# Strassen-like matmul with GELU on one core: the input check moved to settled blocks, transposes that read runs, a GELU issued one row tile later

## The chip, the core and the metric

The kernel runs on one core of a Trainium2 chip. The metric is the device time of one execution in microseconds (us); lower is better. The core has a matrix engine (TensorE, PE), a vector engine (VectorE, DVE), a scalar engine (ScalarE, ACT), GpSimd (POOL) and SyncE (SP). Each works through its own queue in order, and they wait for each other by semaphores. GpSimd and SyncE issue the DMA transfers here: GpSimd the loads, which turn float32 into 16-bit floats on the way, and SyncE the stores.

## The reference

```python
def setup_inputs():
    m, k, n = 4096, 4096, 4096
    return {
        "a": np.random.randn(m, k).astype(np.float32),
        "b": np.random.randn(k, n).astype(np.float32),
    }

def reference(a, b):
    x = np.matmul(a, b)
    return 0.5 * x * (1 + np.tanh(np.sqrt(2 / np.pi) * (x + 0.044715 * x**3)))
```

## The kernel before

`half_path` multiplies in float16 with one level of Winograd's form of Strassen's scheme: A, B and the output are each cut into four quadrants ("11", "12", "21", "22"), and seven products of quadrants or of sums of quadrants (`PRODUCTS`, L30) take the place of eight. If a check of the inputs says that their size does not suit float16, `general_path` (L49) computes everything again in bfloat16; with the inputs here it does not run.

**Groups, products, steps.** The output's quadrants are cut into four row blocks (`mb`) of 512 rows and four column blocks (`nb`) of 512 columns. A pair of them is a group, 16 in all, with `nb` the same from the last group of a row block to the first of the next, so that between them only A's blocks change (`groups`, L259). A group runs products 0 to 6, a product has four steps `q` of a quarter of the inner length, and a step has 16 matmuls: four row tiles `i` by four pieces of 128. So a step is 16 matmuls, a product 64, a group 448. Products 1 to 4 gather in the PSUM banks `accX`, products 0, 5 and 6 in `accY`, one bank for each row tile.

**Operands.** `make_sums` (L244) builds with VectorE, two steps ahead of the matmuls, the sums `aS` and `bS` of quadrants (128x2048, float16) for those products that need sums; there are three buffers of each. `settle` (L309), called behind each row tile of a product's last step, takes the result out. At product 1 `keep` copies the bank to `m5` with ScalarE, VectorE makes y = Y - m5, and `emit` (L296) applies GELU with ScalarE and stores y with SyncE. Product 2 goes on in the same banks, so its first matmul into bank `i` waits for the copy of row tile `i`. At product 5 and 6 VectorE makes y out of bank Y and a kept block, and `emit` follows.

**Loads and turns.** `load_a` (L125) brings 512 rows by 1024 columns of A into one of two staging buffers (`stage`) with four DMAs of 32 partitions; `turn_a` (L137) turns it with one VectorE transpose of 4-byte elements (pairs of float16) into `aT`, reading with a step of four elements, and squares every one of its 16 pieces of 256 columns on ScalarE, with a running sum into `stat_a`: the check of A. So a staging buffer is read by VectorE and by ScalarE. `load_b` (L151) brings 1024 rows by 512 columns of B into `bR` with one DMA of 128 partitions. Every DMA of GpSimd takes one of eight semaphores in turn and waits until the DMA eight before it has landed.

**The order.** It is written out by hand: `at(gi, s, q, fn, ...)` hangs a call ahead of a step (L341), and the loop at L430 issues for each step those calls, the sums of the step two later, and the step's matmuls. The first group's loads and turns are listed at L351 to L367; the later ones come from the loop at L378, B's for the next group in its products 3, 4 and 6, A's for the next row block from product 4 of the row block's last group to product 3 of the next. In the second group of each row block `square_b` squares B's blocks on ScalarE, VectorE adds the squares (`add_squares`), and `weigh_b` takes their largest, smallest and total. In the last row block `ask` gathers the figures to DRAM ahead of product 0 of the group before the last, `answer` brings them back in one row and forms the verdict ahead of product 3 there, and `read` loads it into a register of every engine ahead of product 0 of the last group.

Of the kernel before, what the change touches and what calls it, by code (L numbers as in the profile page):

```python
# [16 lines left out]
P = 128  # L17
Q = 32
# [25 lines left out]
A_LOW, A_RATIO = 2.0**-8, 16.0  # L44
B_LOW, B_RATIO = 2.0**-13, 64.0
# [43 lines left out]
def half_path(  # L89
# [21 lines left out]
    n_seg = M * K // (P * RUN)  # L111
    stat_a = pool.tile([P, n_seg], F32, name="stat_a", tag="stat_a")
    stat_b = pool.tile([P, 3, 2 * NNB], F32, name="stat_b", tag="stat_b")
    segments = iter(range(n_seg))
    checks = iter(range(2 * NNB))

    a_v = a.rearrange("(x mm) (c g r) -> c g mm x r", mm=Q, g=4, r=RUN)
    b_v = b.rearrange("(c p j) n -> c p j n", p=P, j=NJ)
# [18 lines left out]
    def turn_a(mb, quad, c):  # L137
        s = staged.pop((mb, quad, c))
        t = pool.tile([P, NJ // 2, TM * 2], F16, name="aT", tag=f"aT{a_slot[quad]}{c}")
        src = s.bitcast(U32).rearrange("p mb (q jj) -> p jj mb q", q=Q)  # L140
# [3 lines left out]
        for x in range(TM // Q):  # L144
            k = next(segments)
            junk = pool.tile([P, RUN], BF16, name="junk", tag="junk")
            nc.scalar.activation(  # L147
                junk[:, :], s[:, x, :], ACT.Square, accum_out=stat_a[:, k : k + 1]
            )

    def load_b(nb, quad, c):  # L151
        kh, jh = int(quad[0]) - 1, int(quad[1]) - 1
        n0 = jh * NH + nb * NC
        t = pool.tile([P, NJ, NC], F16, name="bR", tag=f"bR{b_slot[quad]}{c}")
        nc.gpsimd.dma_start(out=t[:, :, :], in_=b_v[kh * CH + c, :, :, n0 : n0 + NC])  # L155
        b_tiles[nb, quad, c] = t
# [7 lines left out]
    energy, squares = {}, {}  # L164
    W = 2 * NC

    def square_b(nb, quad, c, h):

        src = b_tiles[nb, quad, c].rearrange("p x y -> p (x y)")[:, h * W : (h + 1) * W]
        half = quad[1]  # L170
        if half not in energy:
            t = energy[half] = pool.tile([P, W], BF16, name="energy", tag=f"energy{half}")
        else:
            t = pool.tile([P, W], BF16, name="square", tag="square", bufs=2)
            squares.setdefault(half, []).append(t)
        nc.scalar.activation(t[:, :], src, ACT.Square)  # L176

    def add_squares():
        for half in squares:
            for t in squares[half]:  # L180
                tt(energy[half], energy[half], t, ALU.add)
        squares.clear()

    def weigh_b():
        for half in sorted(energy):
            k, t = next(checks), energy[half]
            nc.vector.tensor_tensor(out=t[:, :NC], in0=t[:, :NC], in1=t[:, NC:], op=ALU.add)
            for r, op in enumerate((ALU.max, ALU.min, ALU.add)):
                nc.vector.tensor_reduce(
                    out=stat_b[:, r, k : k + 1], in_=t[:, :NC], axis=AX.X, op=op  # L190
                )
        energy.clear()

    def gather():

        s = pool.tile([P, 6], F32, name="seen", tag="seen")
        for r, op in enumerate((ALU.max, ALU.min, ALU.add)):
            nc.vector.tensor_reduce(out=s[:, r : r + 1], in_=stat_a[:, :], axis=AX.X, op=op)
            nc.vector.tensor_reduce(out=s[:, 3 + r : 4 + r], in_=stat_b[:, r, :], axis=AX.X, op=op)
# [4 lines left out]
    def verdict(d):  # L204
# [17 lines left out]
        for f, low, ratio in ((0, A_LOW, A_RATIO), (3, B_LOW, B_RATIO)):  # L222
            for src, bound, op in (
                (f, SQUARE_MAX, ALU.is_le), (f + 1, low, ALU.is_ge), (f + 2, TOTAL_MAX, ALU.is_le)
# [6 lines left out]
                out=v[:, f + 1 : f + 2], in0=v[:, f + 1 : f + 2], scalar1=ratio, scalar2=None, op0=ALU.mult  # L231
# [63 lines left out]

    def emit(gi, i, ih, jh, y, src):  # L296
# [12 lines left out]
    def settle(gi, s, i):  # L309

        X, Y = banks.get(("X", i)), banks.get(("Y", i))
        if s == 1:
            m5 = keep("m5", X, 2)
            y = new_y()
            tt(y, Y, m5, ALU.subtract)
            emit(gi, i, 0, 1, y, y)
# [12 lines left out]
        elif s == 5:  # L329
            y = new_y()  # L330
            tt(y, post.pop(("x1", i)), Y, ALU.subtract)
            emit(gi, i, 1, 0, y, y)
        elif s == 6:
            y = new_y()
            tt(y, Y, post.pop(("x7", i)), ALU.add)
            emit(gi, i, 1, 1, y, y)
# [7 lines left out]
    def load_and_turn(gi, quad, c):  # L344
        load_a(0, quad, c)
        turn_a(0, quad, c)


    first = -AHEAD * QPH
    T0 = -3  # L350
    for c in range(CH):  # L351
        at(0, 0, T0 + 2 * c, load_a, 0, "11", c)
        at(0, 0, T0 + 2 * c, load_b, 0, "12", c)
        at(0, 0, T0 + 2 * c, load_b, 0, "22", c)
        at(0, 0, T0 + 2 * c, turn_a, 0, "11", c)
# [121 lines left out]
```

## Time and profile before

| | |
|---|---|
| median of 3 runs | 1704.69 us (1701.78 to 1706.7) |
| the profiled execution, its own time | 1701.63 us |
| its span | 1700.0 us |
| TensorE matmul, busy | 1580.7 us (93%) |
| VectorE, busy | 1209.1 us (71%) |
| ScalarE, busy | 650.8 us (38%) |
| GpSimd, busy | 172.8 us (10%) |
| packets of the load queue, share of 16 DMA engines | 55.8% |
| mean granted TensorE clock | 0.982 |

A matmul row of the timeline joins many matmuls: its start, its length, what it writes and reads, how many, and in brackets the idle time just before it with what ended that. In a group of instructions (by line, engine, operation and shape) stand the busy time, the mean of one in ns, and the idle time ahead of them. A window's row has the busy time of PE, PEld, DVE, ACT and POOL, then the granted clock, the DMA share and GB/s moved. In rows of a DMA the time is that of its issue; the time to landing stands apart.

### The profile page before, as it was taken

What the parts mean: (1) busy time and instruction counts of PE and PEld (TensorE: products, weight loads), DVE (VectorE), ACT (ScalarE), POOL (GpSimd) and SP (SyncE); (2) the same over time, 40 slices, a digit from 0 to 9 for tenths busy, and PEclk for the clock granted to TensorE, in tenths of its full rate; (3) what the DMA queues carried; (4) which work ended last, traced back from release to release, by engine and by line L of the source; (5) the groups of instructions that cost most, each with busy time, mean ns of one, the idle gap of its engine ahead of it and who ended that gap; (6) DMA issues with size and microseconds to landing.
All of it is one profiled execution on the core that took longest, in us unless ns stands there. A gap on an engine that the chain in (4) does not pass through costs nothing. (4 is left out here: it accounts for less than half of the span.)

```text
span 1700.0 us, 19147 instructions
## 1 busy us (share of the span) xinstructions
PE 1580.7 (93%) x7168; PEld 706.4 (42%) x7168; DVE 1209.1 (71%) x1232; ACT 650.8 (38%) x1602; POOL 172.8 (10%) x236
## 2 busy tenths in 40 slices
PE   3579999999989999999988999999998999999998
PEld 1234444444434444444433444444443444444443
DVE  2657786666868789565797769766577878867575
ACT  4851641211675353111295455121158535311121
POOL 3301000010120001011021100001002110100000
PEclk9779999999999999999999999999999999999999
DMA  9977567684596837479176777747729773777702
GB/s 180 163 120 146 110 124 149 124 171 77 95 142 107 178 75 150 97 126 205 41 120 114 123 152 135 150 91 152 129 50 149 123 154 77 139 150 127 149 25 76
DMA packets 213141, 211.06 MB, mean 124 GB/s; under 512 B 8240, under 2 KB 180272, under 8 KB 213040
## 3 DMA queue, kind: packets, MB, share of 16 engines
q0 software_dynamic: 175744, 142.62, 55.8%
q1 hardware_dynamic: 37296, 67.13, 11.3%
q8 instruction: 58, 0.95, 0.2%
q14 instruction: 43, 0.35, 0.1%
HBM read 285.22 MB, written 67.11 MB: 207 GB/s over the span
## 5 line engine op out<-in xcount | busy, mean ns | idle before, releaser
L280 PEld LDWEIGHTS <-aS 128*128 128x128 f16 x5120 | 503.9, 98 | 689.0 <-issue 82.9
L252 DVE TENSOR_TENSOR aS<-aT 128x2048 f16<-128x2048 f16 x320 | 386.7, 1219 | 196.0 <-PE accX L280 149.3
L280 PE MATMUL accX<-bS,aS 128*128 128x512 f16 x2048 | 459.2, 383 | 44.6 <-ACT m L293 34.1
L252 DVE TENSOR_TENSOR bS<-bR 128x2048 f16<-128x2048 f16 x320 | 387.9, 1218 | 85.4 <-PE accX L280 41.1
L280 PEld LDWEIGHTS <-aT 128*128 128x128 f16 x2048 | 202.6, 99 | 296.8 <-issue 46.2
L280 PE MATMUL accY<-bS,aT 128*128 128x512 f16 x1024 | 233.6, 390 | 42.3 <-DVE bS L252 42.3
L298 ACT ACTIVATE y<-y 128x512 f32<-128x512 f32 x192 | 117.2, 628 | 344.4 <-DVE y L307 344.2
L280 PE MATMUL accX<-bR,aS 128*128 128x512 f16 x1024 | 227.2, 382 | 10.8 <-DVE aS L252 10.8
L280 PE MATMUL accY<-bS,aS 128*128 128x512 f16 x1024 | 227.4, 383 | 9.7 <-DVE y L307 8.2
L147 ACT ACTIVATE junk<-stage 128x256 bf16<-128x256 f16 x512 | 213.2, 416 | 49.1 <-DMA stage<-in_a_dram 33.8
L280 PE MATMUL accX<-bS,aT 128*128 128x512 f16 x1024 | 224.1, 379 | 4.5 <-DVE bS L252 4.5
L280 PE MATMUL accY<-bR,aS 128*128 128x512 f16 x1024 | 223.6, 379 | 0.0
L155 POOL DMA_DIRECT2D bR<-in_b_dram x104 | 90.8, 875 | 999.2 <-DVE bS L252 302.6
L142 DVE STREAM_TRANSPOSE aT<-stage 128x2048 uint32<-128x2048 uint32 x32 | 124.3, 3884 | 63.9 <-DMA stage<-in_a_dram 63.9
L293 ACT COPY x<-accX 128x512 f32<-128x512 f32 x128 | 74.7, 586 | 225.7 <-PE accX L280 225.7
L176 ACT ACTIVATE square<-bR 128x1024 bf16<-128x1024 f16 x120 | 122.5, 1051 | 83.0 <-DVE energy L307 83.0
L131 POOL DMA_DIRECT2D stage<-in_a_dram x128 | 81.9, 648 | 415.7 <-ACT junk L147 355.5
L293 ACT COPY m<-accX 128x512 f32<-128x512 f32 x64 | 36.5, 570 | 198.1 <-PE accX L280 198.1
L147 ACT ACTIVATION_READ_ACCUMULATOR junk<-stage 128x1 f32 x512 | 95.4, 186 | 0.0
L298 ACT ACTIVATE y<-accX 128x512 f32<-128x512 f32 x64 | 38.2, 597 | 131.1 <-PE accX L280 131.1
L307 DVE TENSOR_TENSOR energy<-energy,square 128x1024 bf16<-128x1024 bf16 x120 | 82.3, 686 | 8.5 <-ACT square L176 5.8
L307 DVE TENSOR_TENSOR y<-accY,m 128x512 f32<-128x512 f32 x64 | 44.1, 690 | 59.7 <-ACT m L293 59.7
(22 smaller groups left out, 248.5 us busy)
## 6 DMA issues: line engine op xcount, KB each, us to landing
bR<-in_b_dram POOLq DMA_DIRECT2D x104, 1024.0 KB, 11.8
out_dram<-y SPq DMA_DIRECT2D x256, 256.0 KB, 5.3
stage<-in_a_dram POOLq DMA_DIRECT2D x128, 256.0 KB, 8.2
row<-seen_d SPq DMA_DIRECT2D x2, 1.5 KB, 2.2
seen_d<-seen SPq DMA_DIRECT2D x1, 3.0 KB, 7.4
```

Source lines behind the costliest of these rows:

```text
L131: nc.gpsimd.dma_start(out=s[g * Q : (g + 1) * Q, :, :], in_=a_v[kh * CH + c, g, :, x0 : x0 + TM // Q, :],)
L142: nc.vector.transpose(dst, src)
L147: nc.scalar.activation(junk[:, :], s[:, x, :], ACT.Square, accum_out=stat_a[:, k : k + 1])
L155: nc.gpsimd.dma_start(out=t[:, :, :], in_=b_v[kh * CH + c, :, :, n0 : n0 + NC])
L176: nc.scalar.activation(t[:, :], src, ACT.Square)
L252: nc.vector.tensor_tensor(out=t[:, :], in0=part(tiles, blk, o[0], q), in1=part(tiles, blk, o[1], q), op=ALU.add if o[2] > 0 else ALU.subtract,
L280: nc.tensor.matmul(banks[chain, i][:, :], sa[:, j // 2, i * P : (i + 1) * P, j % 2], sb[:, j, :], start=first and j == 0, stop=q == QPH - ...
L293: nc.scalar.copy(out=t[:, :], in_=src[:, :])
L298: nc.scalar.activation(y[:, :], src[:, :], ACT.Gelu_apprx_tanh)
L307: nc.vector.tensor_tensor(out=o[:, :], in0=x[:, :], in1=y[:, :], op=op)
```

## The change

Four things change. (1) The squares of A no longer read the staging rows. `square` now serves A and B alike: B's blocks are squared in the second group of each row block as before, A's turned blocks in the third; VectorE adds the squares into an `energy` tile for each half, and `weigh` adds its two halves, transposes 32 by 32 blocks and sums runs of 32, with bounds to match. (2) `turn_a` reads runs of 32 four-byte elements; the inner index of the product is thereby numbered in another order, so B's rows go to other partitions and places, and `load_b` issues eight DMAs of 32 partitions for each tile. (3) The GELU and store of a result made by a subtraction or addition are held in `waiting` and issued by `flush` one row tile later, the last one ahead of the next step's matmuls. (4) The first group's loads and turns are listed in another order, with each turn just ahead of the sums that need it, and the check's gathering, verdict and reading move to products 0, 2 and 4 of the last group.

```diff
     def turn_a(mb, quad, c):
...
-        src = s.bitcast(U32).rearrange("p mb (q jj) -> p jj mb q", q=Q)
+        src = s.bitcast(U32).rearrange("p mb (jj q) -> p jj mb q", q=Q)
...
-        for x in range(TM // Q):
-            k = next(segments)
-            junk = pool.tile([P, RUN], BF16, name="junk", tag="junk")
-            nc.scalar.activation(
-                junk[:, :], s[:, x, :], ACT.Square, accum_out=stat_a[:, k : k + 1]
-            )
...
-        nc.gpsimd.dma_start(out=t[:, :, :], in_=b_v[kh * CH + c, :, :, n0 : n0 + NC])
+        for g in range(4):
+            for e in range(2):
+                nc.gpsimd.dma_start(
+                    out=t[g * Q : (g + 1) * Q, e::2, :],
+                    in_=b_v[kh * CH + c, g, e, :, :, n0 : n0 + NC],
+                )
...
+    def weigh(which):
+        for half in sorted(energy):
+            k, t = next(checks[which]), energy[half]
+            pair = t.rearrange("p (m e) -> p e m", e=2) if which == "a" else t.rearrange("p (e m) -> p e m", e=2)
+            u = pool.tile([P, W], BF16, name="square", tag="square", bufs=2)
+            nc.vector.tensor_tensor(out=u[:, :NC], in0=pair[:, 0, :], in1=pair[:, 1, :], op=ALU.add)
+            nc.vector.transpose(u[:, NC:], u[:, :NC])
+            nc.vector.tensor_reduce(
+                out=stats[which][:, k * NX : (k + 1) * NX],
+                in_=u[:, NC:].rearrange("p (x q) -> p x q", q=Q), axis=AX.X, op=ALU.add,
+            )
...
+    waiting = []
+    def flush():
+        for args in waiting:
+            emit(*args)
+        waiting.clear()
...
         if s == 1:
             m5 = keep("m5", X, 2)
+            flush()
             y = new_y()
             tt(y, Y, m5, ALU.subtract)
-            emit(gi, i, 0, 1, y, y)
+            waiting.append((gi, i, 0, 1, y, y))
...
             tt(y, post.pop(("x1", i)), Y, ALU.subtract)
-            emit(gi, i, 1, 0, y, y)
+            flush()
+            waiting.append((gi, i, 1, 0, y, y))
...
+        (-3, ("A11 0", "B12 0", "B22 0", "T11 0", "A11 1", "B12 1", "B22 1")),
+        (0, ("T11 1", "A12 0", "A12 1")),
+        (2, ("T12 0", "A22 0", "B21 0")),
+        (4, ("T12 1", "A22 1", "B21 1", "B11 0")),
+        (6, ("T22 0", "B11 1", "A21 0")),
+        (8, ("T22 1", "A21 1")),
+        (18, ("T21 0",)),
+        (20, ("T21 1",)),
...
-    for mb in range(NMB):
-        gi = mb * NNB + 1
...
+        for which, gi in (("b", mb * NNB + 1), ("a", mb * NNB + 2)):
...
-    at(len(groups) - 2, 0, 0, ask)
-    at(len(groups) - 2, 3, 0, answer)
-    at(len(groups) - 1, 0, 0, read)
+    at(len(groups) - 1, 0, 0, ask)
+    at(len(groups) - 1, 2, 0, answer)
+    at(len(groups) - 1, 4, 0, read)
...
+            flush()
             if n >= 0:
                 multiply(*steps[n])
+        flush()
```

ScalarE at the end of product 1 in the second group (`m` is the copy of a bank, `y` the result under GELU), before:

```order
L176 ACTIVATE square<-bR 128x1024 x15
L293 COPY m_1236<-accX 128x512
L298 ACTIVATE y<-y 128x512
L293 COPY m_1246<-accX 128x512
L298 ACTIVATE y<-y 128x512
L293 COPY m_1256<-accX 128x512
L298 ACTIVATE y<-y 128x512
L293 COPY m_1266<-accX 128x512
L298 ACTIVATE y<-y 128x512
```

and now:

```order
L177 ACTIVATE square<-bR 128x1024 x12
L297 COPY m_1087<-accX 128x512
L297 COPY m_1095<-accX 128x512
L310 ACTIVATE y<-y 128x512
L297 COPY m_1105<-accX 128x512
L310 ACTIVATE y<-y 128x512
L297 COPY m_1115<-accX 128x512
L310 ACTIVATE y<-y 128x512
L177 ACTIVATE square<-bR 128x1024
L310 ACTIVATE y<-y 128x512
```

Each GELU moved behind the next row tile's copy, and the last one behind a square of the next step.

VectorE at the program's start, from its first transpose (`aT` is a turned A block, `bS` and `aS` are sums), before:

```order
L142 STREAM_TRANSPOSE aT<-stage 128x2048
L252 TENSOR_TENSOR bS<-bR 128x2048
L142 STREAM_TRANSPOSE aT<-stage 128x2048
L252 TENSOR_TENSOR bS<-bR 128x2048 x2
L142 STREAM_TRANSPOSE aT<-stage 128x2048
L252 TENSOR_TENSOR bS<-bR 128x2048
L252 TENSOR_TENSOR aS<-aT 128x2048
L142 STREAM_TRANSPOSE aT<-stage 128x2048
L252 TENSOR_TENSOR aS<-aT 128x2048 x2
```

and now:

```order
L143 STREAM_TRANSPOSE aT<-stage 128x2048
L256 TENSOR_TENSOR bS<-bR 128x2048 x2
L143 STREAM_TRANSPOSE aT<-stage 128x2048
L256 TENSOR_TENSOR bS<-bR 128x2048 x2
L143 STREAM_TRANSPOSE aT<-stage 128x2048
L256 TENSOR_TENSOR aS<-aT 128x2048 x2
L143 STREAM_TRANSPOSE aT<-stage 128x2048
L256 TENSOR_TENSOR aS<-aT 128x2048 x2
```

The second and third transposes each moved behind one more sum of B: those of steps 1 and 3 now stand ahead of the turns that steps 2 and 4 need.

SyncE over the whole program (`out` are the stores of y, `seen_d` and `row` carry the check's figures), before:

```order
L301 DMA out_dram<-y 128x512 x224
L201 DMA seen_d<-seen 128x6
L301 DMA out_dram<-y 128x512 x4
L210 DMA row<-seen_d 1x128x3 x2
L301 DMA out_dram<-y 128x512 x12
L421 TENSOR_LOAD flag
L301 DMA out_dram<-y 128x512 x16
```

and now:

```order
L313 DMA out_dram<-y 128x512 x239
L205 DMA seen_d<-seen 128x6
L313 DMA out_dram<-y 128x512 x4
L214 DMA row<-seen_d 1x128x3 x2
L313 DMA out_dram<-y 128x512
L431 TENSOR_LOAD flag
L313 DMA out_dram<-y 128x512 x12
```

The check's transfers moved by 15 stores towards the end: of the last group's 16 stores three (one more is left over from the group before) now stand between `seen_d` and `row`, and the fourth store of product 1 stands behind `row`.

More of the change, by code (lines that the diff above doesn't have):

```diff
@@ L174, in square_b @@
             t = pool.tile([P, W], BF16, name="square", tag="square", bufs=2)
[L175 removed]
+            squares.append((half, t))
         nc.scalar.activation(t[:, :], src, ACT.Square)
     def add_squares():
[L179 to L181 removed]
+        for half, t in squares:
+            tt(energy[half], energy[half], t, ALU.add)
         squares.clear()
[L184 removed]
+    def weigh(which):
         for half in sorted(energy):
[L186 to L191, printed above, removed]
+            k, t = next(checks[which]), energy[half]
[7 more added lines that the diff above has]
+            )
         energy.clear()
```

82 lines of the change are left out of this document (36 added, 46 removed).

## The prediction

> **What bounds the kernel now.** I read the page's busy shares first, then the timeline of TensorE, then, for every place where TensorE waits, the engine it waits for. TensorE is busy 93% of the span. Its timeline (start, length, engine, line, operation, count, and in brackets the wait before) shows three kinds of loss. A product is 64 matmuls and four steps; a group is seven products.
>
> ```profile
> span 1700.0 us, 19147 instructions
> ```
> ```profile
> 296.96 1.92 PE L280 MATMUL accX<-bS,aS 128*128 128x512 f16 x8
> 299.72 1.02 PE L280 MATMUL accX<-bS,aS 128*128 128x512 f16 x4 [0.84 <-ACT m L293]
> 301.58 25.20 PE L280 MATMUL accX<-bS,aS 128*128 128x512 f16 x116 [0.84 <-ACT m L293]
> 326.61 13.98 PE L280 MATMUL accX<-bS,aT 128*128 128x512 f16 x64
> 340.42 13.98 PE L280 MATMUL accY<-bR,aS 128*128 128x512 f16 x64
> ...
> 395.68 1.92 PE L280 MATMUL accX<-bS,aS 128*128 128x512 f16 x8
> ...
> 455.74 7.07 PE L280 MATMUL accY<-bS,aS 128*128 128x512 f16 x32 [2.62 <-DVE y L307]
> ...
> 474.68 15.66 PE L280 MATMUL accY<-bS,aT 128*128 128x512 f16 x64 [3.63 <-DVE bS L252]
> ...
> 506.08 1.27 PE L280 MATMUL accX<-bS,aS 128*128 128x512 f16 x5
> ...
> 606.46 1.71 PE L280 MATMUL accX<-bS,aS 128*128 128x512 f16 x6
> ```
>
> Rows 326.61 and 340.42 are 13.81 us apart: one undisturbed product, 3.45 us a step. Seven are 96.7. From product 2 of one group to product 2 of the next an ordinary group takes 395.68 - 296.96 = 98.7, so 2.0 are lost, and the brackets say where: at product 2, twice, on a copy by ScalarE. The group in which new A tiles arrive takes 506.08 - 395.68 = 110.4, which is 11.7 more than an ordinary one, and the group behind it 606.46 - 506.08 = 100.4, 1.7 more. There are three such pairs, one for each later row block, and the other two look alike in the timeline. The third loss is the start:
>
> ```profile
> 22.62 6.45 PE L280 MATMUL accY<-bS,aT 128*128 128x512 f16 x16 [22.62 <-DVE bS L252]
> 32.52 4.93 PE L280 MATMUL accY<-bS,aT 128*128 128x512 f16 x16 [3.44 <-DVE bS L252]
> 38.27 3.61 PE L280 MATMUL accY<-bS,aT 128*128 128x512 f16 x16 [0.82 <-DVE bS L252]
> 47.65 5.89 PE L280 MATMUL accY<-bS,aT 128*128 128x512 f16 x16 [5.76 <-DVE bS L252]
> ...
> 81.82 1.87 PE L280 MATMUL accX<-bS,aS 128*128 128x512 f16 x4 [8.45 <-ACT m L293]
> ...
> 170.40 4.91 PE L280 MATMUL accY<-bS,aT 128*128 128x512 f16 x22
> ```
>
> Group 0 runs from 22.6 to 170.4: 147.8 us for 96.7 of work. The rows also show that a step after a pause runs slowly: 5.9 to 6.5 us after a long one against 3.6 after 0.82.
>
> **The change, part by part.**
>
> *GELU one row tile later.* ScalarE at the end of product 1:
>
> ```profile
> 393.29 0.58 ACT L293 COPY m<-accX 128x512 f32<-128x512 f32 x1 [23.62 <-PE accX L280]
> 395.42 0.63 ACT L298 ACTIVATE y<-y 128x512 f32<-128x512 f32 x1 [1.55 <-DVE y L307]
> 395.95 0.57 ACT L293 COPY m<-accX 128x512 f32<-128x512 f32 x1
> ```
>
> The GELU stands ahead of the next copy and waits 1.55 us for VectorE's subtraction; the copy that frees the next bank is queued behind it. In the new order two copies come first, then GELU and copy alternate. From these rows: copies 0 and 1 end at 393.9 and 394.7, GELU 0 cannot start before 395.4, so copy 2 ends at about 396.6 and copy 3 at 397.7. TensorE, without waits, wants banks 2 and 3 at 395.68 + 1.73 = 397.4 and at 398.3. Both are in time, by 0.6 us or more. The wait goes from groups 1 to 15: 15 x 2.0 = **-30**. At products 5 and 6 the deferral only shifts a GELU past instructions that free no bank; I cost it at nothing, since no copy is queued there (a late GELU would hold one of four output buffers).
>
> *Squares off the staging rows, transposes in runs.* What A's arrival waits for is read at GpSimd (POOL), which issues the loads, and at VectorE, which turns them; both views are of the start, and a third groups the durations (busy us, mean ns of one, idle before):
>
> ```profile
> 36.50 2.54 POOL L131 DMA_DIRECT2D stage<-in_a_dram  x4 [11.39 <-ACT junk L147]
> 51.57 2.54 POOL L131 DMA_DIRECT2D stage<-in_a_dram  x4 [12.52 <-ACT junk L147]
> ```
> ```profile
> 36.99 1.23 DVE L252 TENSOR_TENSOR bS<-bR 128x2048 f16<-128x2048 f16 x1 [4.52 <-DMA bR<-in_b_dram]
> 42.67 3.81 DVE L142 STREAM_TRANSPOSE aT<-stage 128x2048 uint32<-128x2048 uint32 x1 [4.46 <-DMA stage<-in_a_dram]
> ```
> ```profile
> L142 DVE STREAM_TRANSPOSE aT<-stage 128x2048 uint32<-128x2048 uint32 x32 | 124.3, 3884 | 63.9 <-DMA stage<-in_a_dram 63.9
> L176 ACT ACTIVATE square<-bR 128x1024 bf16<-128x1024 f16 x120 | 122.5, 1051 | 83.0 <-DVE energy L307 83.0
> ...
> L307 DVE TENSOR_TENSOR energy<-energy,square 128x1024 bf16<-128x1024 bf16 x120 | 82.3, 686 | 8.5 <-ACT square L176 5.8
> ...
> L307 DVE TENSOR_TENSOR y<-accY,m 128x512 f32<-128x512 f32 x64 | 44.1, 690 | 59.7 <-ACT m L293 59.7
> ...
> L198 DVE TENSOR_REDUCE seen<-stat_a 128x1 f32<-128x512 f32 x3 | 2.0, 675 | 0.0
> ...
> L199 DVE TENSOR_REDUCE seen<-stat_b 128x1 f32<-128x8 f32 x3 | 0.4, 149 | 0.0
> ```
>
> A staging buffer is free again only when 16 squares (junk) have read it, and the next load waits for that, 11.4 and 12.5 us here; now the transpose alone frees it. No row shows a 4-byte transpose that reads runs. Its upper end is the 3.88 us of the strided one. For the lower: the two reductions of contiguous 4-byte data give (675 - 149) / 504 = 1.04 ns an element, so 149 + 2040 x 1.04 = 2.3 us for 2048. I take 2.3, an estimate, since contiguous 4-byte reading is what those rows have in common with it. The Trainium skill ("Vector Engine (DVE) Microarchitecture Reference", Measured stream behaviour) has 1.75 ns a column for a port that steps every element and 1.054 in runs of two words or more; the trace's 1.90 is near the first, and no run here shows the second.
>
> Where A arrives (three times): loads now start when a transpose ends, so VectorE's waits for staged data (63.9 us in all, the transpose's row) go, and with them the waits for sums such as that at 474.68. What is late next is VectorE itself: in the 12 steps of products 5, 6 and 0 stand six transposes, 16 sums of 1.23 and eight results of 0.69, together 48 us at 3.88 a transpose and 39 at 2.3, against 41.4 of matmuls. With 2.3 nothing is left; with 3.88 the wait of 2.62 on y stays, some 1.5 behind it, and most of the 1.7 of the next group, where two more transposes stand among sums. So -3 x (11.7 + 1.7) = -40, of which I leave 2 for what I have overlooked: **-38** (at 3.88: -3 x 8 = -25).
>
> The new squares of A stand in the third group of each row block: 32 x 1051 ns on ScalarE, which hides beside matmuls, and 30 adds x 686 ns plus two weighings (each an add, a transpose and a reduction of 512, about 2 us by the rows above) on VectorE, 25 us.
>
> ```profile
> 198.02:296.96 98.94, 97.18 (x450) 43.85 (x448) 76.24 (x89) 32.89 (x45) 6.97 (x8) 1.00 0.66 128
> 296.96:395.68 98.72, 97.05 (x450) 43.82 (x449) 62.38 (x64) 16.55 (x29) 12.13 (x16) 1.00 0.83 149
> ```
>
> VectorE (third pair) goes there from 62 to about 87 of 96.7 us. The first row is the group that squares B, built alike, at 76 with its first adds just ahead of the window; TensorE lost nothing more in it. So nothing, and if that cover fails, the overrun alone, a few us four times.
>
> *The start.* At 20 to 40 us the DMA engines moved 201 GB/s (1.05 MB a tile: 5.2 us), and the rows at 36.99 and 42.67 waited for data, not for ScalarE.
>
> ```profile
> 20.00:40.00 20.00, 13.12 (x41) 4.91 (x41) 7.39 (x4) 9.88 (x40) 5.12 (x8) 0.91 1.34 201
> ```
>
> So the first seven tiles land as before, the seventh at 42.7; from there I add 5.2 a tile, since squares no longer hold the loads: A12's second tile at 47.9, A22's first at 53.4 (its buffer is free at 45.0), then B21 58.6, A22 63.9, B21 69, B11 74.3 and 79.5, A21 by 90. TensorE: product 0 to 47.3 (its third step slow after a pause), product 1 to 61.1; product 2 has its first sums at 60 and starts at 61.1 in place of 81.8; its third step has its sum at 70.4, 2.5 late, and costs some 1.5 of slow clock; product 3 starts at 78.5 and nothing is late behind it: 78.5 + 4 x 13.8 + 1 = 135 against 170.4, **-35**. Not under 22.6 + 96.7 = 119 in any case (-51), and at worst 0.
>
> Each B tile now has 8 issues on GpSimd for one. Rows of the tiles bR and stage:
>
> ```profile
> L155 POOL DMA_DIRECT2D bR<-in_b_dram x104: 873/873/887, 4.1 to 1587.2; - x104
> ...
> DMA to landing us min/median/max: 7.8/11.8/24.8
> ```
> ```profile
> L131 POOL DMA_DIRECT2D stage<-in_a_dram x128: 642/642/779, 1.4 to 1318.8; - x128
> ...
> DMA to landing us min/median/max: 3.8/8.2/26.2
> ```
>
> An issue costs 873 ns with 1024 pieces and 642 with 512; a line through them gives 0.47 us at 128, so 3.8 a tile, under the 5.2 of its data. At most 0.873: 7.0 a tile, 1.8 more, and by the sixth B tile +11 at the start. I take 0.47, nearest to the stage row, which has the same 32 partitions. Eight may be in flight; one alone would land in about 3.1 us (3.8 and 7.8 for 256 and 1024 KB, in line), so eight cover 5.2 us.
>
> *The check's end.* Its SyncE transfers move from behind a product boundary's outputs in a group with slack to between the third and fourth output of product 1 of the last group.
>
> ```profile
> 1529.16 1.23 SPq L210 DMA_DIRECT2D row<-seen_d  x2
> ```
> ```profile
> 1537.62 1.47 DVE L216 TENSOR_REDUCE v<-row 1x1 f32<-1x128 f32 x6
> ```
> ```profile
> row<-seen_d SPq DMA_DIRECT2D x2, 1.5 KB, 2.2
> ```
>
> The verdict is next on VectorE, with the sums of two steps later queued behind it. With T the end of product 1: third GELU T + 1.9, second row transfer lands T + 5.3, verdict (the six reductions of its row, 1.47, and twelve smaller operations behind them, about as long) T + 8.1, two sums T + 10.5; wanted at T + 6.9: **+3.6** (0 to 6).
>
> Sum on the profiled execution, 1701.6 (span 1700.0 and 1.6 around it): 1701.6 - 30 - 38 - 35 + 3.6 = 1602. The median shown, 1704.7, is 3 above that execution, so I say 1605.
>
> **The rivals.**
> (a) Transposes stay at 3.88: -25 in place of -38, and 2 more at the start: 1620. For it: only their reading changes. Against it: 1.90 ns an element is far above what contiguous rows have.
> (b) The split loads are slower than one: 7 us a B tile, 1616 to 1620 with the restart of the clock.
> (c) Copies of product 1 still late, in the groups with squares: half of the 30 stays, 1620.
> (d) Slower than before: the eighths do not overlap. 3.1 us each, one behind the other, is 25 a tile and 200 for a group's eight tiles, against 96.7 of matmuls: twelve groups lose 100 each, about 2800. It decides from about 12 us a tile (96.7 / 8) and ends above the old time from 13.1. Against it: four pieces of A are issued in 2.54 us (row 36.50) while none lands in under 3.8, so they do overlap, and 201 GB/s were reached with them. The Trainium skill ("DMA: Bandwidth & Descriptors", Rules for kernel authors) is for this rival: 128 partitions and at least 1 MiB a DMA, and transfers to disjoint partitions serialize; with its fixed 2 us a piece would make a tile near 20 us, an estimate from that page; the stage rows, 256 KB to 32 partitions, do not bear it out.
> (e) The start gains nothing: 1640.
>
> **How the numbers follow.** Forecast 60% (1592 to 1612), a 13%, b 11%, c 6%, e 5%, d 2%, and 3% for other things of either sign. The range 1590 to 1638 takes in a, b and c. Within 0.3% (5 us, about what can be told from no change) 2%, slower 3%, faster 95%.
>
> **What would show it.** Products 1 and 2 join without a wait on m; the transpose row near 2.3 us; groups with new A near 97; no square on stage; product 2 of group 0 at 61 and group 1 at 135; a wait of some 3.6 us of TensorE in product 2 of the last group, behind bS or aS. Wrong would be: POOL busy above 700 us, B tiles that sums wait for in ordinary groups, or VectorE waits in every third group.

## The result and the profile after

| | before | after |
|---|---|---|
| median of 4 runs | 1704.54 us (1701.78 to 1706.7) | 1604.4 us (1601.1 to 1605.89) |
| after against before | | 0.9411 (95%: 0.939 to 0.9432) |
| the profiled execution, its own time | 1701.63 us | 1601.1 us |
| its span | 1700.0 us | 1599.4 us |
| TensorE matmul, busy | 1580.7 us (93%) | 1554.7 us (97%) |
| VectorE, busy | 1209.1 us (71%) | 1243.0 us (78%) |
| ScalarE, busy | 650.8 us (38%) | 517.6 us (32%) |
| GpSimd, busy | 172.8 us (10%) | 530.8 us (33%) |
| packets of the load queue, share of 16 DMA engines | 55.8% | 61.1% |
| mean granted TensorE clock | 0.982 | 0.996 |

The changed kernel is faster by 5.9%, at 1604.4 us where 1605 was predicted. These are pieces of TensorE's timeline after, with the same columns as before: product 2 of group 0, the start of group 1, product 2 of groups 2 to 5, and the last group from its product 2.

```profile
61.66 1.89 PE L284 MATMUL accX<-bS,aS 128*128 128x512 f16 x8
64.68 5.48 PE L284 MATMUL accX<-bS,aS 128*128 128x512 f16 x24 [1.13 <-ACT m L297]
74.16 22.57 PE L284 MATMUL accX<-bS,aS 128*128 128x512 f16 x96 [4.00 <-DVE bS L256]
...
138.00 13.98 PE L284 MATMUL accY<-bS,aT 128*128 128x512 f16 x64
...
262.32 27.79 PE L284 MATMUL accX<-bS,aS 128*128 128x512 f16 x128
...
359.01 27.79 PE L284 MATMUL accX<-bS,aS 128*128 128x512 f16 x128
...
455.70 27.79 PE L284 MATMUL accX<-bS,aS 128*128 128x512 f16 x128
...
552.49 27.79 PE L284 MATMUL accX<-bS,aS 128*128 128x512 f16 x128
...
1519.60 7.07 PE L284 MATMUL accX<-bS,aS 128*128 128x512 f16 x32
1530.10 20.88 PE L284 MATMUL accX<-bS,aS 128*128 128x512 f16 x96 [3.43 <-DVE bS L256]
```

Products 2 and 3 now run as one row of 128 matmuls with no bracket. From product 2 to product 2 an ordinary group takes 359.01 - 262.32 = 96.69, seven undisturbed products. The group in which new A tiles arrive takes 455.70 - 359.01 = 96.69 as well (before: 110.40), and the group behind it 96.79 (before: 100.38). Group 0 ends at 138.00 in place of 170.40. What TensorE still waits for is the start and one wait of 3.43 us in the last group.

The groups of instructions on the other engines (count, busy us, mean ns of one, idle before and what ended it):

```profile
L152 POOL DMA_DIRECT2D bR<-in_b_dram x832 | 448.6, 544 | 720.2 <-DVE bS L256 357.8
...
L319 DVE TENSOR_TENSOR energy<-energy,square 128x1024 bf16<-128x1024 bf16 x240 | 164.6, 686 | 10.1 <-ACT square L177 6.4
...
L143 DVE STREAM_TRANSPOSE aT<-stage 128x2048 uint32<-128x2048 uint32 x32 | 73.8, 2306 | 27.0 <-DMA stage<-in_a_dram 26.9
```

The transpose takes 2306 ns for 3884. Its waits for staged data sum to 27.0 us, from 63.9. The adds of squares have doubled, 240 for 120, and the issues of B tiles take 544 ns each, 448.6 us of GpSimd in all.

**Where the 100.5 us went.** The span cut at product 2 of groups 1 and 15 (198.02 and 1621.47 before; 165.63 and 1519.60 after):

| stretch | before | after | difference | made of |
|---|---|---|---|---|
| start to product 2 of group 1 | 198.02 | 165.63 | -32.4 | the start |
| from there to product 2 of group 15 | 1423.45 | 1353.97 | -69.5 | 14 x 2.03 = 28.4 by the GELU's place; the other 41.1 where A arrives (40.2 by the differences of those six groups) |
| from there to the end | 78.53 | 79.80 | +1.3 | -2.0 by the GELU's place, +3.4 by the verdict |

The sum is -100.6 of span; the executions' own times differ by 100.5.

### The profile page after: what moved, and what is told of

Read it like the earlier page. It is cut to its first block, busy times and chain, and to the rows that moved or that the text cites. A ratio compares the mean times of both kernels' runs of the same rounds, so it can differ in the third digit from the quotient of the medians.

```text
span 1599.4 us, 19504 instructions
## 1 busy us (share of the span) xinstructions
PE 1554.7 (97%) x7168; PEld 702.9 (44%) x7168; DVE 1243.0 (78%) x1368; ACT 517.6 (32%) x706; POOL 530.8 (33%) x964
## 3 DMA queue, kind: packets, MB, share of 16 engines
q0 software_dynamic: 187392, 142.67, 61.1%
## 5 line engine op out<-in xcount | busy, mean ns | idle before, releaser
L152 POOL DMA_DIRECT2D bR<-in_b_dram x832 | 448.6, 544 | 720.2 <-DVE bS L256 357.8
L284 PE MATMUL accX<-bS,aS 128*128 128x512 f16 x2048 | 446.9, 380 | 8.6 <-DVE bS L256 7.4
L284 PE MATMUL accY<-bS,aT 128*128 128x512 f16 x1024 | 228.5, 385 | 29.1 <-DVE bS L256 29.1
L284 PE MATMUL accX<-bR,aS 128*128 128x512 f16 x1024 | 223.6, 379 | 0.0
L284 PE MATMUL accY<-bS,aS 128*128 128x512 f16 x1024 | 223.6, 379 | 0.0
L319 DVE TENSOR_TENSOR energy<-energy,square 128x1024 bf16<-128x1024 bf16 x240 | 164.6, 686 | 10.1 <-ACT square L177 6.4
L177 ACT ACTIVATE square<-aT 128x1024 bf16<-128x1024 f16 x120 | 123.9, 1051 | 64.6 <-DVE energy L319 64.3
L143 DVE STREAM_TRANSPOSE aT<-stage 128x2048 uint32<-128x2048 uint32 x32 | 73.8, 2306 | 27.0 <-DMA stage<-in_a_dram 26.9
L319 DVE TENSOR_TENSOR x<-accX,x 128x512 f32<-128x512 f32 x64 | 44.3, 692 | 43.0 <-ACT y L310 43.0
```

The source lines that it names most:

```text
L143: nc.vector.transpose(dst, src)
L152: nc.gpsimd.dma_start(out=t[g * Q : (g + 1) * Q, e::2, :], in_=b_v[kh * CH + c, g, e, :, :, n0 : n0 + NC],)
L284: nc.tensor.matmul(banks[chain, i][:, :], sa[:, j // 2, i * P : (i + 1) * P, j % 2], sb[:, j, :], start=first and j == 0, stop=q == QPH - ...
L319: nc.vector.tensor_tensor(out=o[:, :], in0=x[:, :], in1=y[:, :], op=op)
```

## The experiments

Each edit is made to the changed kernel, except in the two that are made to the kernel before, and each is set against runs of the kernel before on the same chip.

**The GELU issued at once again.**

```diff
-            flush()
-            waiting.append((gi, i, 0, 1, y, y))
+            emit(gi, i, 0, 1, y, y)
```

(and likewise at products 5 and 6)

> The changed kernel with the GELU and store of a sum issued at once again. Theory (the GELU ahead of the next copy held the bank): the two waits of 0.84 us on m come back at product 2 of groups 1 to 15, 2.0 us a group, so about 1604 + 30 = 1634, and product 2 to product 2 is 98.7 again. Rival (the copies were late because ScalarE was full of squares and running sums, which stay away here): the waits stay gone or shrink below 0.3 us, 1604 to 1612.

Measured: 1633.87 us, 0.9587 (0.9571 to 0.9603), 29.5 above the changed kernel. TensorE's timeline of this run, product 2 of group 2:

```profile
266.05 1.02 PE L284 MATMUL accX<-bS,aS 128*128 128x512 f16 x4 [0.84 <-ACT m L297]
267.92 25.20 PE L284 MATMUL accX<-bS,aS 128*128 128x512 f16 x116 [0.84 <-ACT m L297]
```

The two waits of the kernel before are back at their old size, in groups 1 to 15. The term was 30.4, and taking the part away costs 29.5.

**The kernel before with nothing but the later GELU** (the `waiting` list and `flush` put into it).

> The kernel before with the GELU one row tile later and nothing else. Theory (the gain of this part stands by itself): product 2 to product 2 falls from 98.7 to 96.7 in the ordinary groups, 30 us in all, 1674 (1668 to 1678), the start and the three groups with new A as before. Rival (in the old kernel the squares on ScalarE keep the copies late): 10 us or less, 1694.

Measured: 1671.25 us, 0.9803 (0.9784 to 0.9821), 34.3 below its kernel before (1705.53). Ordinary groups take 96.69; group 0 ends at 171.58, and where A first arrives waits of 2.62, 3.65, 1.65 and 1.49 us remain (2.62, 1.17, 3.63, 1.92 and 1.50 in the kernel before). So this part works by itself, and the other losses stay. The size is known only to a few us: 34.3 by the medians, 27.3 between the two profiled executions (1701.63 and 1674.32), around the 30.4 of the term.

**Transposes with a step of four again** (the split loads of B kept).

```diff
-        src = s.bitcast(U32).rearrange("p mb (jj q) -> p jj mb q", q=Q)
+        src = s.bitcast(U32).rearrange("p mb (q jj) -> p jj mb q", q=Q)
```

> The changed kernel with transposes that read with a step of four elements again, B still loaded as now, so that the inner indices of A and B no longer match: the same work, another product. Theory (where A arrives VectorE has just enough time with 2.3 us a transpose and too little with 3.88): in the three groups that turn A a wait of about 2.6 us on y and 1.5 behind it, 1.5 in the next group, so 3 x 5.6 = 17 and 2 at the start: 1623. Rival (free staging buffers alone removed those waits): only the start moves, by 2 to 3: 1607.

Measured: 1624.62 us, 0.9534 (0.9518 to 0.955), 20.2 above the changed kernel. TensorE's timeline where A first arrives, and the transpose's group:

```profile
420.12 7.07 PE L284 MATMUL accY<-bS,aS 128*128 128x512 f16 x32 [2.58 <-DVE y L319]
427.97 7.07 PE L284 MATMUL accY<-bS,aS 128*128 128x512 f16 x32 [0.78 <-DVE bS L256]
...
498.94 7.07 PE L284 MATMUL accX<-bS,aT 128*128 128x512 f16 x32 [1.49 <-DVE bS L256]
```
```profile
L143 DVE STREAM_TRANSPOSE aT<-stage 128x2048 uint32<-128x2048 uint32 x32 | 124.0, 3874 | 18.7 <-DMA stage<-in_a_dram 18.7
```

The theory held, and the rival with its 1607 did not. The wait of 2.58 on y stays, as the prediction had it for 3.88 us, with 0.78 and 1.49 behind it. From product 2 to product 2 these waits and what follows them cost 5.5, 5.5 and 5.7 in the three places (in the first 3.9 in the group where A arrives and 1.6 in the next), 16.7 in all. Group 0 ends at 141.12, 3.1 later. The slow transposes keep VectorE busy for 50.2 us more (124.0 for 73.8), of which some 20 appear in the time: those at the start and in the three places where six transposes stand among 16 sums.

**The squares back on the staging rows.**

```diff
     def turn_a(mb, quad, c):
...
+        for x in range(TM // Q):
+            k = next(segments)
+            junk = pool.tile([P, RUN], BF16, name="junk", tag="junk")
+            nc.scalar.activation(junk[:, :], s[:, x, :], ACT.Square, accum_out=stats["a"][:, k : k + 1])
...
-        for which, gi in (("b", mb * NNB + 1), ("a", mb * NNB + 2)):
+        for which, gi in (("b", mb * NNB + 1),):
```

> The changed kernel with A checked on the staging rows again (16 squares with running sums for each tile behind its transpose) and no squares of A in the third groups. Theory (a staging buffer held by ScalarE delays the next load): the loads where A arrives go out about every 10.5 us in place of every 7, VectorE waits for staged data again, 6 to 9 us lost in each of the three groups and about 15 to 20 at the start: 1640 (1630 to 1650). Rival (the slow transposes made those waits, and with 2.3 us there is room for the late loads): 1604 to 1612.

Measured: 1639.14 us, 0.9612 (0.9595 to 0.963), 34.7 above the changed kernel. TensorE's timeline from product 2 of group 3 to that of group 4, and the end of group 0:

```profile
141.77 13.98 PE L292 MATMUL accY<-bS,aT 128*128 128x512 f16 x64
...
362.78 27.79 PE L292 MATMUL accX<-bS,aS 128*128 128x512 f16 x128
...
428.15 8.53 PE L292 MATMUL accY<-bS,aS 128*128 128x512 f16 x32 [3.05 <-DVE bS L264]
...
437.26 13.97 PE L292 MATMUL accY<-bS,aT 128*128 128x512 f16 x64 [0.58 <-DVE bS L264]
...
458.34 12.22 PE L292 MATMUL accX<-bR,aS 128*128 128x512 f16 x48 [3.65 <-DVE aS L264]
470.40 14.84 PE L292 MATMUL accX<-bS,aS 128*128 128x512 f16 x68
```

The total is the 1640 that was expected, but by luck. The group takes 470.40 - 362.78 = 107.6, 10.9 above 96.7, and the other two 12.5 and 9.2 above it, where 6 to 9 were expected; the start loses only 141.77 - 138.00 = 3.8, where 15 to 20 were expected. With the new listing the squares on the staging rows thus cost the start little. That left the listing of the first group as a suspect.

**The old listing of the first group**: the loops of the kernel before in place of the table.

```diff
-        (-3, ("A11 0", "B12 0", "B22 0", "T11 0", "A11 1", "B12 1", "B22 1")),
-        (0, ("T11 1", "A12 0", "A12 1")),
...
+    for c in range(CH):
+        at(0, 0, c, load_a, 0, "12", c)
+        at(0, 0, 1 + 2 * c, turn_a, 0, "12", c)
...
+    for c in range(CH):
+        at(0, 1, 2 + c, load_a, 0, "21", c)
+        at(0, 2, 1 + 2 * c, turn_a, 0, "21", c)
```

> The changed kernel with the first group's loads and turns listed in the old order. Theory (most of the start's 32 us comes from free staging buffers and the listing only places a turn ahead of sums that could go first): group 0 ends 4 to 8 us later, 1608 to 1612, and product 0's last step starts near 47 in place of 42. Rival (the listing itself made the start): 15 us or more, 1620 and up. Other rival: no difference, 1604.

Measured: 1620.78 us, 0.951 (0.9492 to 0.9529), 16.4 above the changed kernel; group 0 ends at 155.09, 17.1 later. The theory fell: not 4 to 8, and the rival, the listing itself, is right. The reason stands in the timelines of TensorE and of VectorE in this run:

```profile
72.84 11.06 PE L284 MATMUL accX<-bS,aS 128*128 128x512 f16 x40 [7.20 <-ACT m L297]
94.89 18.92 PE L284 MATMUL accX<-bS,aS 128*128 128x512 f16 x80 [10.99 <-DVE bS L256]
...
155.09 13.98 PE L284 MATMUL accY<-bS,aT 128*128 128x512 f16 x64
```
```profile
90.28 2.31 DVE L143 STREAM_TRANSPOSE aT<-stage 128x2048 uint32<-128x2048 uint32 x1 [13.50 <-DMA stage<-in_a_dram]
```

In the old listing the first turn of A21 stands in VectorE's queue ahead of the sums of product 2, though only product 5 needs it. Its tile is among the last loaded. VectorE stands 13.50 us at it, with the sums queued behind it, and TensorE waits 10.99 us for them.

**The old listing with only A21's turns later**, to test that reading.

```diff
-        at(0, 2, 1 + 2 * c, turn_a, 0, "21", c)
+        at(0, 4, 2 + 2 * c, turn_a, 0, "21", c)
```

> The changed kernel with the old order at the start, but A21's two turns ahead of the sums of product 5 as in the new one. Theory (of the 17 us that the old order costs, 11 to 13 are the turn of A21's first tile, at which VectorE stood 13.5 us waiting for data ahead of the sums of product 2): group 0 ends at 141 to 145 in place of 155, 1608. Rival (the other turns, too early as well, cost as much): 150 or later, 1616.

Measured: 1606.15 us, 0.9421 (0.9407 to 0.9435). Group 0 ends at 141.50: of the 17.1 us that the old listing costs, these two calls alone give back 13.6.

**The kernel before with nothing but the new listing.**

> The kernel before with the first group's loads and turns in the new order and nothing else. Theory (the old order's cost is VectorE waiting at a turn whose data has not come, with sums behind it that could go, and the squares only delay that data further): group 0 ends at 145 to 150 in place of 170.4, 1680 to 1685. Rival (in the old kernel the squares on the staging rows make the start late whatever the order): 165 or later, 1699 and up.

Measured: 1681.19 us, 0.9863 (0.9848 to 0.9879), 23.6 below its kernel before (1704.82). Group 0 ends at 145.60 in place of 170.40: with the squares on the staging rows and the slow transposes still there, the listing alone brings 24.8 us of the start. TensorE's rows of this run at product 2 of group 0 and at the start of group 1, the row that begins group 1 in the run ahead of it, and GpSimd's rows of this run:

```profile
70.31 1.87 PE L280 MATMUL accX<-bS,aS 128*128 128x512 f16 x4 [8.36 <-ACT m L293]
...
145.60 13.98 PE L280 MATMUL accY<-bS,aT 128*128 128x512 f16 x64
```
```profile
141.50 8.80 PE L284 MATMUL accY<-bS,aT 128*128 128x512 f16 x40
```
```profile
36.06 2.54 POOL L131 DMA_DIRECT2D stage<-in_a_dram  x4 [11.04 <-ACT junk L147]
51.46 2.54 POOL L131 DMA_DIRECT2D stage<-in_a_dram  x4 [12.86 <-ACT junk L147]
```

GpSimd's long waits for the squares are still there, 11.04 and 12.86 us where the kernel before has 11.39 and 12.52.

**One DMA of 128 partitions for each B tile**, B's rows in their old order.

```diff
-        for g in range(4):
-            for e in range(2):
-                nc.gpsimd.dma_start(
-                    out=t[g * Q : (g + 1) * Q, e::2, :],
-                    in_=b_v[kh * CH + c, g, e, :, :, n0 : n0 + NC],
-                )
+        nc.gpsimd.dma_start(out=t[:, :, :], in_=b_v[kh * CH + c, :, :, n0 : n0 + NC])
```

> The changed kernel with one DMA of 128 partitions for each B tile, rows in the old order, so that the inner indices of A and B no longer match: the same work, another product. Theory (eight pieces with eight semaphores pass the slow rhythm of an A load on and leave the DMA engines half idle at 66 to 74 us of the changed kernel's trace): the wait of 4.0 us in product 2 of group 0 shrinks to 1 or less, group 0 ends 3 to 5 us earlier, 1600; later groups stay as they are. Rival (pieces cost nothing, the bytes set the start): group 0 ends within 1 us of 138.0, 1604.

Measured: 1601.14 us, 0.9391 (0.9376 to 0.9407); the interval overlaps that of the changed kernel, so the 0.2% between the medians, the price of eight issues for one, is not told apart from none. Group 0 ends at 134.80, 3.2 earlier, and the third step of product 2 waits 0.30 in place of 4.00:

```profile
72.65 20.88 PE L279 MATMUL accX<-bS,aS 128*128 128x512 f16 x96 [0.30 <-DVE bS L251]
...
134.80 13.98 PE L279 MATMUL accY<-bS,aT 128*128 128x512 f16 x64
```

The size is as expected. The cause that went with it, DMA engines half idle in the changed kernel while that step waits, is not there, and no other is shown. The windows of the changed kernel ahead of and around the wait, columns as before:

```profile
40.00:60.00 20.00, 20.00 (x86) 8.69 (x85) 13.58 (x9) 0.59 (x1) 10.07 (x18) 0.91 1.28 178
60.00:68.00 8.00, 6.87 (x32) 2.96 (x31) 7.11 (x8) 5.14 (x8) 5.45 (x11) 1.00 1.33 188
68.00:74.00 6.00, 2.16 (x11) 0.88 (x9) 2.92 (x3) 0.00 (x0) 2.60 (x5) 1.00 1.14 277
74.00:82.00 8.00, 7.84 (x29) 3.26 (x29) 6.72 (x7) 1.17 (x2) 6.50 (x12) 0.79 1.24 202
```

The engines moved more at 68 to 74 us than beside it, 277 GB/s: four stores of 256 KB, of the results of product 1, run there along with the loads.

**The verdict one product later.** In the last group the answer stands ahead of product 3 and the reading ahead of product 5.

```diff
-    at(len(groups) - 1, 2, 0, answer)
-    at(len(groups) - 1, 4, 0, read)
+    at(len(groups) - 1, 3, 0, answer)
+    at(len(groups) - 1, 5, 0, read)
```

> The changed kernel with the verdict one product later in the last group (ahead of product 3, read ahead of product 5). Theory (the row transfers behind a waiting store and the small operations behind them hold the sums of product 2): the wait of 3.4 us in product 2 of the last group goes, 1601, with no new wait. Rival (VectorE is only moved to be late in product 3, where eight results follow): 1604.

Measured: 1600.21 us, 0.9388 (0.9371 to 0.9406). The wait of 3.43 us in product 2 of the last group is gone and no other takes its place. The median falls by 4.2; as the interval just overlaps that of the changed kernel, the gain rests on the trace. The two runs below keep this edit.

**A third staging buffer at the start**: the first tile of A22 is staged in a buffer that B11 takes later.

```diff
-        s = pool.tile([P, TM // Q, RUN], F16, name="stage", tag="stage", bufs=2)
+        if (mb, quad, c) == (0, "22", 0):
+            s = pool.tile([P, NJ, NC], F16, name="stage", tag="bR31")
+            s = s.rearrange("p j (h r) -> p (j h) r", r=RUN)
+        else:
+            s = pool.tile([P, TM // Q, RUN], F16, name="stage", tag="stage", bufs=2)
```

> The verdict one product later, and at the start A22's first tile staged in a buffer of B that is loaded later, so that its load need not wait for the transpose of A12's first tile. Theory (loads of A gated by transposes leave the DMA engines short at 46 and 58 us): product 2 of group 0 gets its sums 2 to 4 us earlier, group 0 ends at 134 to 136, 1598. Rival (the rhythm of eight pieces sets it, whatever the order): group 0 ends at 138, 1601.

Measured: 1598.65 us, 0.9378 (0.936 to 0.9395). The theory fell: group 0 ends at 140.29, against 139.42 in the run with the later verdict alone, and the third step of product 2 waits longer, not less (3.62 in that run, behind a sum that starts at 74.30; here 74.56):

```profile
75.84 23.17 PE L288 MATMUL accX<-bS,aS 128*128 128x512 f16 x96 [5.87 <-DVE bS L260]
```

So the wait for a staging buffer is no longer what holds the start.

**The first group's stores of product 1 held back to product 3.**

```diff
         if s == 1:
...
-            waiting.append((gi, i, 0, 1, y, y))
+            if gi == 0:
+                at(0, 3, 2, emit, gi, i, 0, 1, y, y)
+            else:
+                waiting.append((gi, i, 0, 1, y, y))
```

> The verdict one product later, and the GELUs and stores of product 1 of group 0 held until product 3 (step 14). Theory (the four stores, 1 MB, take a good part of the DMA engines at 68 to 74 us, just when B21's second tile is awaited): its sum comes 2 to 3 us earlier, the wait of 3.6 to 4.0 in product 2 of group 0 shrinks to about 1, group 0 ends at 135 to 136 in place of 138 to 139, 1597. Rival (the pace of eight pieces sets that tile's landing): no change against the kernel with the later verdict alone, 1600.

Measured: 1596.84 us, 0.9369 (0.9356 to 0.9382), the shortest of all. Its timeline at that step, at the end of group 0 and in the last group, and the window of the stores:

```profile
73.26 22.55 PE L284 MATMUL accX<-bS,aS 128*128 128x512 f16 x96 [3.56 <-DVE bS L256]
...
137.09 13.98 PE L284 MATMUL accY<-bS,aT 128*128 128x512 f16 x64
...
1518.68 27.79 PE L284 MATMUL accX<-bS,aS 128*128 128x512 f16 x128
```
```profile
68.00:74.00 6.00, 2.44 (x10) 0.94 (x9) 4.34 (x4) 0.00 (x0) 5.03 (x10) 0.94 1.18 178
```

The wait of the last group is absent here too: its products 2 and 3 are one row. Without the stores the window moves 178 GB/s, all of it loads; with them it moved 277, of which the four stores can be at most 1.05 MB / 6 us = 175. So there is more room for loads there, and the sum starts earlier: by 0.9 against the changed kernel (71.98 for 72.88), by 2.3 against the run with the later verdict (74.30), from which this one differs by the stores alone. Group 0 ends 2.3 earlier than in that run (137.09 for 139.42). That would fit the theory's 2 to 3, but the two kernels with the stores in place differ by 1.4 themselves. The wait did not shrink to 1 as expected: TensorE also arrives earlier and still waits 3.56 us. This version's interval lies wholly below that of the changed kernel, 7.6 us by the medians. The verdict's wait of 3.4 is a part of it that the trace shows; what holding the stores adds can't be told apart from none, as the intervals of the last three runs overlap.

## Why the prediction was right, and the step that was wrong

The sum held to about 1 us, while single terms were off by up to 3.1 and cancelled: the arrival of A brought 3.1 more than forecast, the start 2.6 less, the other two were off by 0.4 or less. That the total fits so closely is luck in this part.

**The GELU, -30.** Measured 15 x (98.72 - 96.69) = 30.4. The order of ScalarE's queue after, at the end of product 1 of group 2:

```profile
259.93 0.59 ACT L297 COPY m<-accX 128x512 f32<-128x512 f32 x1 [3.90 <-PE accX L284]
260.79 0.59 ACT L297 COPY m<-accX 128x512 f32<-128x512 f32 x1 [0.27 <-PE accX L284]
262.06 0.63 ACT L310 ACTIVATE y<-y 128x512 f32<-128x512 f32 x1 [0.68 <-DVE y L319]
262.60 0.57 ACT L297 COPY m<-accX 128x512 f32<-128x512 f32 x1
263.06 0.63 ACT L310 ACTIVATE y<-y 128x512 f32<-128x512 f32 x1
263.59 0.58 ACT L297 COPY m<-accX 128x512 f32<-128x512 f32 x1
```

The third copy ends at 263.17 and the fourth at 264.17. TensorE begins product 2 at 262.32 and wants their banks at 264.05 and 264.9: both in time, by 0.9 and 0.7, as worked out. Rival (c), half of the waits kept, did not come. Removing this part and doing it alone agree with the term (29.5 and 34.3).

**Where A arrives, -38.** Measured 41.1 (what is left of that stretch without the GELU's 28.4), a little more than the 40 at which nothing is left. The estimate of 2.3 us for the transpose, on which this term stood, was met by 2306 ns. Both edits were needed, and the runs price them: with the squares back on the staging rows 10.9, 12.5 and 9.2 us return in the three groups. With the strided transposes 5.5 to 5.7 return at each, close to the 5.4 that the prediction left for them (13.4 less 8; its 3 x 8 is 24, where it wrote 25), and the whole comes to 1624.6, where rival (a) had 1620. The Trainium skill ("Vector Engine (DVE) Microarchitecture Reference", Measured stream behaviour) agrees in size: its 1.75 ns a column, with both sources stepping at every element, against 1.054 is a difference of 0.70 ns a column, and this case has (3884 - 2306) / 2048 = 0.77.

**The squares of A in the third group, 0.** Right: VectorE's 120 more adds of 686 ns lie beside matmuls, and product 2 to product 2 is 96.69 there.

**The start, -35.** The size was nearly right, 32.4, and the reason was wrong in good part. This is the step that failed: "from there I add 5.2 a tile, since squares no longer hold the loads". The loads came close to that (A12's second tile, A22's first and B21's first were used from 47.63, 53.95 and 59.39; 47.9, 53.4 and 58.6 predicted), but most of the gain does not hang on the squares' hold on the loads. The end of group 0 in the runs:

| kernel | group 0 ends |
|---|---|
| before | 170.40 |
| before, with the new listing alone | 145.60 |
| changed, with the squares back on the staging rows | 141.77 |
| changed, with the strided transposes back | 141.12 |
| changed | 138.00 |
| changed, with the old listing | 155.09 |
| changed, with the old listing but A21's turns late | 141.50 |

The listing, which has no term in the sum, brings 24.8 when it alone is done and 17.1 when it alone is undone. So the rest of the change (the squares, the transposes, the split loads, the GELU) brings 7.6 beside the new listing, of which 3.8 and 3.1 return when the squares and the transposes are undone one at a time, but 170.40 - 155.09 = 15.3 beside the old one. The shares depend on the order, and how the 15.3 divide was not run.

The prediction read the waits of 11.4 and 12.5 us on GpSimd as time that the start would gain. They were real, but the loads behind them were mostly not the next thing that TensorE needed: with the new listing alone these waits are as long as ever, and group 0 ends 24.8 earlier. The new order of the turns was known and shown ahead of the prediction, which gave it no term of its own; what it would have taken is to ask, at each turn of the old order, what stands queued behind it. In the changed kernel with the old listing the answer is the 13.50 us at A21's first turn. In the kernel before it is spread out. There 11.5 of the 24.8 are lost ahead of product 2, which starts at 81.82 in place of 70.31. Then come these rows of TensorE and VectorE in that kernel:

```profile
101.59 6.22 PE L280 MATMUL accX<-bS,aS 128*128 128x512 f16 x16 [4.79 <-DVE bS L252]
113.23 15.89 PE L280 MATMUL accX<-bS,aS 128*128 128x512 f16 x64 [5.42 <-ACT x L293]
```
```profile
95.45 3.84 DVE L142 STREAM_TRANSPOSE aT<-stage 128x2048 uint32<-128x2048 uint32 x1 [4.56 <-DMA stage<-in_a_dram]
```

VectorE stands 4.56 us at A21's first turn, and TensorE waits 4.79 for a sum behind it. It then waits 5.42 for copies by ScalarE, behind the squares of A21's two tiles, which run from 95.44 to 112.61. In that kernel a turn brings its squares into ScalarE's queue, so the old listing puts those too ahead of what TensorE needs. What each turn costs in that kernel was not tested.

What is left of the start against the prediction is 138.0 - 135 = 3.0. Product 2 starts at 61.66 (61.1 predicted). It then loses 1.13 on m, which the prediction did not have, and its third step starts at 74.16 in place of 70.4, after a wait of 4.00 for a sum. This is VectorE's row of that sum:

```profile
72.88 1.22 DVE L256 TENSOR_TENSOR bS<-bR 128x2048 f16<-128x2048 f16 x1 [2.98 <-DMA bR<-in_b_dram]
```

It waits for B21's second tile, which the prediction had there at 69. Why that tile comes some 3.9 us later stays partly open. The 5.2 a tile stand on 201 GB/s; at 40 to 60 us the engines moved 178, which over 20 us is about 2.3 us of loads, an estimate from these two rates. Neither the third staging buffer nor one DMA a tile changes that rate much (182 and 180 GB/s at 40 to 60 us). Holding the stores brings the sum 0.9 to 2.3 forward, by the kernel against which it is set. With one DMA a tile the sum starts at 71.37, but TensorE then arrives later too, at a lower granted clock (0.78 at 66 to 73 us, where the changed kernel has 1.00), so that run does not settle it. Two kernels with the same start (the changed one and the one with the later verdict) end group 0 at 138.00 and 139.42, so differences of a microsecond or two at the start are not to be read closely.

**The verdict, +3.6.** Measured 3.43, behind bS in product 2 of the last group, as worked out. SyncE's and VectorE's rows there:

```profile
1522.43 1.22 SPq L214 DMA_DIRECT2D row<-seen_d  x2
```
```profile
1524.58 0.31 DVE L220 TENSOR_REDUCE v<-row 1x1 f32<-1x128 f32 x1 [2.40 <-DMA row<-seen_d]
...
1527.71 1.20 DVE L256 TENSOR_TENSOR aS<-aT 128x2048 f16<-128x2048 f16 x1
1528.84 1.21 DVE L256 TENSOR_TENSOR bS<-bR 128x2048 f16<-128x2048 f16 x1
```

VectorE stands 2.40 us at the row's landing and spends 3.13 on the verdict; the two sums queued behind end at 1530.05, and TensorE goes on at 1530.10. One product later the same work hides.

**The issues on GpSimd.** 0.544 us for one, where the line through 873 and 642 gave 0.47: the cost falls less below 512 pieces than above. At 4.4 us a tile it is still under the 5.2 of its data. The rivals (b) and (d) did not come. The rule of the Trainium skill ("DMA: Bandwidth & Descriptors", Rules for kernel authors), 128 partitions and at least 1 MiB a DMA, is not borne out in the time of this kernel: pieces of 128 KB to 32 partitions take a median of 5.3 us to land with eight in flight, and one DMA a tile gives an overlapping interval. Only in group 0 did the trace with one DMA a tile end 3.2 us earlier.

## What to carry to other kernels

On an engine that works in order, an instruction that waits for a load belongs just ahead of its first use, since everything queued behind it waits as well: the two turns of one block, listed too early, cost 13.6 us in the changed kernel, and one GELU ahead of a copy that frees a bank 2 us in each group. A long wait in the profile is a gain only if what it delays is the next thing the bottleneck lacks, so ask of each wait who is behind it. A sum that comes out right does not prove its terms: undo each part by itself, and do it alone, before naming its share. Where the two differ, as 17.1 and 24.8 do for the listing, the share depends on what else is there.

## What the runs showed of the hardware

A 4-byte transpose of 128x2048 costs 1.68 times as much when it reads with a step of four elements (3884 ns, 1.90 ns an element) as when it reads runs of 32 (2306 ns, 1.13 ns an element), with as many elements written.

Splitting each of 104 loads into eight added 187392 - 175744 = 11648 packets to the load queue, which is 16 for each of the 728 additional DMAs, beside nearly the same bytes (142.62 and 142.67 MB):

```profile
q0 software_dynamic: 187392, 142.67, 61.1%
```

At 20 to 40 us, loads alone ran at 201 GB/s before, with one DMA a B tile, and at 197 after, with eight. With stores beside them 277 GB/s went through the same DMA engines, so loads alone did not reach what these engines can move.
